# A decoder trunk on eight cores: engine orders and PSUM banks from a list schedule, and a packed layout from the host

## The chip, the cores and the metric

One Trainium2 chip, all 8 of its cores (two dies of four). Each core runs the same program on one prompt of 2048 tokens and on 16 sample sequences of 8 tokens; the cores do not talk to each other. The metric is the device time of the slowest core in microseconds, over separate executions. In the views PE is TensorE (matmuls), PEld its weight loads, DVE VectorE, ACT ScalarE, POOL GpSimd and SP SyncE; PSUM is the memory that PE writes to (`psum` in the views); both programs divide it into eight banks of 512 f32 columns.

## The reference, cut to what matters

Four layers. In each, `h` is a modulated RMS norm of `x`:

```python
def swiglu(h, wg, wu, wd):                    # 1024 -> 2816 -> 1024, twice per layer
    return (silu(h @ wg) * (h @ wu)) @ wd

def token_mixer(h, ...):                      # between the two FFNs
    xp, xl, gl, u, v, gates = split(h @ w_in) # 1024, 1024, 1024, 512, 512, 3 x 1024 wide
    y_pool = pool_mixer(xp)       # running means of 2, 4, 8, 16 tokens minus xp, times 256x256 blocks
    xc     = causal_conv(xl)      # 4 taps per channel
    y_lru  = rg_lru(xc) * gelu(gl)# two 128x128 gates per head, sigmoid, exp, sqrt(1 - a^2), a scan in time
    y_gm   = u * spatial_gate(v)  # RMS norm of v, then 128x128 causal mixing of positions
    g = sigmoid(gates)
    merged = g0*(y_pool @ wbo_pool) + g1*(y_lru @ wbo_lru) + g2*(y_gm @ wbo_gmlp)
    return merged @ w_out

mod = silu(c) @ w_ada + b_ada     # 9 x 1024 modulation values per layer (adaLN), 17 columns per core
```

The new pooling, convolution and recurrent states, and the normed `v` of the samples, are outputs too. The tokens go in two groups: group A is two prompt tiles of 512 tokens, group B two more and the sample tile of 128.

## The kernel before

Weights come from HBM as f32 and are cast to bf16 into a ring of 4 slots. A recorder works out semaphores from overlapping reads and writes; **each engine runs its operations in the order in which the code recorded them**, so the code itself is the schedule. What matters of it:

```python
class Sched:
    def add(self, eng, fn, reads=(), writes=(), dma=False):
        ...                              # dependencies from 512-byte pages last written and read
        self.ops[eng].append(o)          # the engine's order is the recorded order

psrot = {"mm": [0, 1, 2, 3], "aux": [4, 5], "tr": [6, 7]}   # PSUM banks, three rotations
def ps(pool="mm"): ...                   # the next bank of that rotation
SCRW = 10240
scr = sb("scr", [P, SCRW])               # one scratch area, cut by hand at fixed offsets

def lru_A(ch, t, par, wxl, wgl, wr_, wi_):   # one recurrent unit: a channel block of a tile
    U = BASE + par * 3344                # par = unit number % 2: two fixed scratch sets
    ...                                  # xl matmuls, 5 conv operations, the cast xcb, gl matmuls
    def stage_b():                       # put off by ONE unit, by hand
        mm(pr, wr_, xcb); mm(pi, wi_, xcb)     # the two gate matmuls that need the cast
        ...                              # gelu, tanh, tanh, exp, exp, ln, exp, two products, scan
        tt(ybr[:, ch, cols], xcf, gel, ALU.mult)
    return stage_b

# in mixer(): three branches one after the other, all through the buffer ybr
#   pooling -> gate_merge(0) -> recurrence -> gate_merge(1) -> gMLP -> gate_merge(2) -> w_out
def store_rows(src_fn, ncols, dram_rows):    # states go out as rows: transposed on PE
    for kb in range(2):
        for k4 in range(4): tr(pt[0:ncols, ...], src_fn(kb * 4 + k4))
        act(stg[...], pt[0:ncols, :], AF.Copy)
    dma(dram_rows, stg[0:ncols, :])

def wload(parts):                        # at EVERY weight load (group A, in the FFNs) ...
    ...
    if ada_hook[0] is not None: ada_hook[0]()   # ... one adaLN block of 2 MB (as f32) is loaded and used too
```

## Time and profile before

| | before |
|---|---|
| runs ahead of the change, us | 10006, 10009, 10119 |
| span of the profiled execution, us | 9312.5 |
| PE busy, share of the span | 78% |
| floor of PE's work (worked out in the prediction), us | 6670 |

Read it so: PE's own work is 6670 us and the span is 9312, so some 2640 us are the time in which PE waits, runs at a lower granted clock (0.52 in the second window of the start, 0.75 and 0.77 in two recurrent windows), or transposes. The prediction below shows the head of the page, the windows and the waits. Only the DMA lines are added here, from the page of the kernel before (packets by size; then for the queue of weight loads packets, MB, and the time that its packets took as a share of 16 engines' span):

```profile
DMA packets 1057984, 581.21 MB, mean 62 GB/s; under 512 B 301317, under 2 KB 1047469, under 8 KB 1057418
...
q0 software_dynamic: 974976, 536.94, 44.5%
```

More than nine packets in ten belong to the queue of weight loads; they are rows of weight blocks, 1 KB or less as written in bf16 (536.94 MB in 974976 packets, 551 bytes in the mean).

### The profile page before, as it was taken

The numbers are of one execution on the slowest core, as the hardware profiler recorded it, in microseconds if no ns is written. First come the engines' busy times: TensorE is split into PE (matmuls) and PEld (weight loads), VectorE is DVE, ScalarE is ACT, GpSimd is POOL, SyncE is SP. The second block draws the span as 40 slices with busy tenths as digits, with TensorE's granted clock in tenths as the row PEclk, the third lists the DMA queues.
The fourth block names the chain that finished last, engine by engine and source line by source line (L and its number), as shares of the span: only waits on it lengthen the run. The fifth ranks groups of instructions, "written<-read, shape, count | busy, mean of one in ns | idle before, by whom it ended". The sixth has DMA issues, their size and how long they took to land.

```text
span 9312.5 us, 113738 instructions; the slowest of 8 cores (9178.1 to 9312.5 us)
## 1 busy us (share of the span) xinstructions
PE 7283.7 (78%) x38120; PEld 3496.2 (38%) x38854; DVE 3499.0 (38%) x6164; ACT 2885.6 (31%) x4619; POOL 891.6 (10%) x1076
## 2 busy tenths in 40 slices
PE   2976888679976898696865699866898667996688
PEld 1422443234432343243432344433444333443344
DVE  0254223632155223632236232354323453324632
ACT  2143222521234222522126122254222452223621
POOL 1110111101110110110001010010000100110000
PEclk7988999889988999897987899988999888997899
DMA  4833886336942654354433254322544323543233
GB/s 82 115 47 49 114 115 91 48 54 84 123 54 42 83 70 54 50 67 81 47 53 35 45 63 59 52 36 41 66 58 56 44 43 53 66 54 50 39 53 62
DMA packets 1057984, 581.21 MB, mean 62 GB/s; under 512 B 301317, under 2 KB 1047469, under 8 KB 1057418
## 3 DMA queue, kind: packets, MB, share of 16 engines
q0 software_dynamic: 974976, 536.94, 44.5%
q1 hardware_dynamic: 82442, 36.95, 1.7%
q8 instruction: 327, 5.36, 0.2%
q14 instruction: 239, 1.96, 0.1%
HBM read 1095.39 MB, written 15.25 MB: 119 GB/s over the span
## 4 chain that ended last, share of the span: by engine, by line
PE 64%; DVE 13%; ACT 7%; DMA 6%; issue 6%; another core or an unknown queue 2%; DVEq 0%; POOL 0%; ACTq 0%; SPq 0%; POOLq 0%
PE psum L327 63%; ACT scr L345 6%; DVE scr L361 5%; DMA ring<-w_ada 4%; DVE scr L348 4%; DVE scr L365 2%; ACT L345 1%; PE psum L333 1%; DVE scr L375 1%; DVE scr L356 1%; DMA scr<-xp 0%; DVEq L180 0%; DMA ring<-w_out 0%; DMA o_pool_s<-stg 0%
## 5 line engine op out<-in xcount | busy, mean ns | idle before, releaser
L327 PE MATMUL psum<-hT,ring 128*128 128x512 bf16 (+1 forms) x21972 | 4499.3, 362 | 395.5 <-DMA ring<-w_in 124.3
L327 PEld LDWEIGHTS psum<-hT,ring 128*128 128x128 bf16 x22400 | 2092.1, 102 | 2695.0 <-issue 772.0
L345 ACT ACTIVATE scr<-psum 128x512 f32<-128x512 f32 (+5 forms) x1941 | 998.8, 516 | 4319.4 <-PE psum L327 3905.5
L327 PE MATMUL psum<-merged,ring 128*128 128x512 bf16 (+1 forms) x6253 | 1306.0, 354 | 96.7 <-DVE scr L348 43.4
L327 PE MATMUL psum<-ybr,ring 128*128 128x512 bf16 (+1 forms) x5030 | 1150.5, 355 | 80.8 <-issue 38.6
L348 DVE TENSOR_TENSOR merged<-scr,psum 128x512 bf16<-128x512 f32 (+1 forms) x640 | 388.8, 608 | 1614.1 <-PE psum L327 1596.4
L327 PEld LDWEIGHTS psum<-merged,ring 128*128 128x128 bf16 x6400 | 594.4, 101 | 714.8 <-issue 129.7
L361 DVE SCALAR_TENSOR_TENSOR xT<-psum,modT,xT 128x512 f32<-128x512 f32 x640 | 474.3, 749 | 957.3 <-PE psum L327 957.3
L327 PE MATMUL psum<-scr,ring 128*128 128x512 bf16 (+1 forms) x598 | 200.2, 437 | 752.4 <-DVE scr L365 462.4
L327 PEld LDWEIGHTS psum<-ybr,ring 128*128 128x128 bf16 x5120 | 480.0, 100 | 589.5 <-issue 126.5
L345 ACT ACT_TABLE_LOAD x387 | 496.5, 1283 | 403.8 <-PE psum L327 356.9
L361 DVE SCALAR_TENSOR_TENSOR scr<-scr,psum 128x512 f32<-128x512 f32 x320 | 194.0, 606 | 714.0 <-PE psum L327 499.5
L382 POOL DMA_DIRECT2D ring<-ffn_w_gate x192 | 168.1, 876 | 2771.2 <-PE psum L327 2771.2
L345 ACT ACTIVATE scr<-xT 128x4096 bf16<-128x4096 f32 (+1 forms) x65 | 201.7, 3104 | 658.2 <-DVE xT L361 620.0
L348 DVE TENSOR_TENSOR scr<-xT,scr 128x512 f32<-128x512 f32 (+1 forms) x396 | 250.1, 701 | 404.3 <-ACT scr L345 404.3
L327 PEld LDWEIGHTS psum<-scr,ring 128*128 128x128 bf16 x640 | 60.3, 104 | 862.0 <-issue 844.7
L382 POOL DMA_DIRECT2D ring<-w_in x224 | 200.0, 895 | 1836.0 <-PE psum L327 1716.8
L348 DVE TENSOR_TENSOR ybr<-scr,psum 128x512 bf16<-128x512 f32 (+1 forms) x240 | 145.8, 608 | 597.7 <-PE psum L327 596.0
L361 DVE SCALAR_TENSOR_TENSOR scr<-scr 128x512 f32<-128x512 f32 (+3 forms) x400 | 280.5, 701 | 166.6 <-ACT scr L345 144.2
L361 DVE SCALAR_TENSOR_TENSOR scr<-scr,vecT 128x512 f32<-128x512 f32 (+1 forms) x480 | 322.3, 671 | 53.9 <-DVE scr L361 0.9
L327 PE MATMUL psum<-scr,onesb 128*128 128x512 bf16 (+1 forms) x509 | 150.4, 458 | 200.4 <-ACT scr L345 199.7
L345 ACT ACTIVATE hT<-scr,modT 128x512 bf16<-128x512 f32 x384 | 276.0, 801 | 44.2 <-DVE scr L348 44.2
(86 smaller groups left out, 3675.0 us busy)
## 6 DMA issues: line engine op xcount, KB each, us to landing
ring<-ffn_w_down POOLq DMA_DIRECT2D x128, 704.0 KB, 7.3
ring<-ffn_w_gate POOLq DMA_DIRECT2D x160, 512.0 KB, 6.5
ring<-ffn_w_up POOLq DMA_DIRECT2D x160, 512.0 KB, 8.7
ring<-w_ada POOLq DMA_DIRECT2D x72, 1024.0 KB, 14.0
ring<-w_in POOLq DMA_DIRECT2D x64, 1024.0 KB, 9.5
ring<-w_in POOLq DMA_DIRECT2D x128, 256.0 KB, 5.1
ring<-w_in POOLq DMA_DIRECT2D x32, 512.0 KB, 5.7
ring<-wbo_pool POOLq DMA_DIRECT2D x16, 1024.0 KB, 8.3
```

The lines of the kernel that those rows point to most:

```text
L327: S.add("pe", lambda e: e.matmul(out, lhsT=lhsT, rhs=rhs, start=start, stop=stop), reads=[lhsT, rhs], writes=[out])
L333: S.add("pe", lambda e: e.transpose(out, in_, idn), reads=[in_, idn], writes=[out])
L345: S.add("act", lambda e: e.activation(out=out, in_=in_, func=func, **kw), reads=rd, writes=wr)
L348: S.add(eng, lambda e: e.tensor_tensor(out=out, in0=in0, in1=in1, op=op), reads=[in0, in1], writes=[out])
L356: S.add(eng, lambda e: e.tensor_scalar(out=out, in0=in0, scalar1=s1, scalar2=s2, op0=op0, op1=op1), reads=rd, writes=[out])
L361: S.add(eng, lambda e: e.scalar_tensor_tensor(out=out, in0=in0, scalar=scalar, in1=in1, op0=op0, op1=op1), reads=rd, writes=[out])
L365: S.add(eng, lambda e: e.tensor_copy(out=out, in_=in_), reads=[in_], writes=[out])
L375: S.add("dve", lambda e: e.tensor_tensor_scan(out=out, data0=d0, data1=d1, initial=init, op0=ALU.mult, op1=ALU.add), reads=rd, writes=[out])
L382: fn = lambda e: e.dma_start(out=out, in_=in_)
```

## The change

The intent is to stop ordering engines by hand. The code still records operations, but each has a modelled cost, a whole accumulation is one PE operation, a PSUM bank is a placeholder, and a list scheduler plays the graph through and lets each engine take what is ready first. Around it, the mixer's recording mixes the branches, and the host does all layout. Its core, with cuts:

```diff
+class PV:                       # a PSUM value; its bank is bound while scheduling
+    bank = None; refs = 0
 class Sched:
+    DMA_BW, PE_LAT, SEM_LAT, TABLE, PATIENCE = 215.0, 210.0, 70.0, 1300.0, 5000.0
+    def schedule(self):         # event-driven list schedule, priority = recorded order
+        banks = list(range(8))
+        ...
+                    if e == "pe":    # first ready op; one that needs a new bank only if > 2 are free,
+                        ...          # or if it is the oldest one that still needs a bank
+                            if o.alloc is None or len(banks) > 2 or (banks and o is pending_alloc[pa]):
+                                pick = o
+                    elif e == "act": # first ready op that needs no other activation table,
+                        ...          # unless the oldest has waited over PATIENCE ns
+                    if o.alloc is not None:
+                        o.alloc.bank = banks.pop(0)
+                    self.ops[e].append(o)
-psrot = {"mm": [0, 1, 2, 3], "aux": [4, 5], "tr": [6, 7]}
-scr = sb("scr", [P, SCRW])
+sbufs = [sb("s%d" % i, [P, SBW]) for i in range(NSB)]     # 14 scratch buffers, handed round when freed
+merged, ybr, ylr = RB                                     # the recurrence writes to its own ylr

 def lru_unit(l, ch, t, wblk):
-    return stage_b                   # no putting off by hand any more
-    cp(xlc[:, :, 3:L], pb[...])
+    act(xl[:, :, 3:L], pb(...), AF.Copy)                  # some copies go from DVE to ACT
-    tt(ybr[:, ch, cols], xcf, gel, ALU.mult)
+    tt(ylr[:, ch, t.cols], xcf, gb.f(n), ALU.mult)

 def mixer(...):
+    for c, f in fg:                  # fg: pooling, gates 0, gMLP, gates 2, each with an estimated cost c
+        while i < len(lru_seq) and al / tot_l <= af / tot_f * 1.04:
+            lru_seq[i][1]()          # recurrent units spread among them in proportion
+            ...
+        f()
+    ...                              # gates 1 (on ylr), then w_out

 def ffn(...):
-    for half in range(2): ...        # down projection in two halves of 11, two residual additions
+    acc(py.c(n), [(w[:, j, :], hid(j)[:, t.cols]) for j in range(22)], n)
+    norms[id(t)].chunk(m)            # squares for the next norm, chunk by chunk

+ada_ctl["every"] = 2 if l == 0 else 3     # an adaLN block at every 2nd or 3rd weight load
-    tr(...)                               # all PE transposes of x, states and outputs
+def pack_weights(inp): ...                # host: every weight block as one contiguous row per partition
```

## The prediction

> **What bounds the kernel now.** I read the page first: its head, the busy times and the chain that ended last.
>
> ```profile
> span 9312.5 us, 113738 instructions; the slowest of 8 cores (9178.1 to 9312.5 us)
> ...
> PE 7283.7 (78%) x38120; PEld 3496.2 (38%) x38854; DVE 3499.0 (38%) x6164; ACT 2885.6 (31%) x4619; POOL 891.6 (10%) x1076
> ...
> PE 64%; DVE 13%; ACT 7%; DMA 6%; issue 6%; another core or an unknown queue 2%; DVEq 0%; POOL 0%; ACTq 0%; SPq 0%; POOLq 0%
> ```
>
> No engine but PE is near full, yet PE is only 64% of the chain: the rest is PE waiting. To see where, I read the busy time by windows of 100 us (columns: PE, PEld, DVE, ACT, POOL busy with counts, granted clock, DMA share, GB/s).
>
> ```profile
> 100.00:200.00 100.00, 12.56 (x207) 7.51 (x208) 10.26 (x18) 27.70 (x47) 7.01 (x8) 0.52 0.46 62
> ...
> 1100.00:1200.00 100.00, 86.87 (x554) 40.73 (x563) 17.76 (x25) 16.16 (x40) 17.70 (x20) 0.91 0.98 132
> ...
> 2800.00:2900.00 100.00, 53.29 (x163) 19.64 (x166) 72.71 (x125) 72.04 (x88) 4.62 (x6) 0.75 0.28 43
> ...
> 3200.00:3300.00 100.00, 99.53 (x457) 45.30 (x464) 23.58 (x33) 11.84 (x20) 12.60 (x14) 1.00 0.62 76
> ...
> 6200.00:6300.00 100.00, 49.07 (x213) 23.26 (x219) 77.41 (x171) 80.04 (x111) 7.93 (x11) 0.77 0.24 26
> ```
>
> Four regimes. The first 200 us hardly compute. An FFN stage without disturbance (3200) is perfect: 464 weight loads in 100 us, 215.5 ns for each 512-column matmul, clock 1.00. An FFN stage with adaLN weights beside it (1100) is held by DMA: share 0.98 at 132 GB/s. The recurrent stage (2800, 6200) runs DVE and ACT at 72 to 80% in one dependent chain; PE starves, and its clock falls to 0.75. The waits name the partners:
>
> ```profile
> PE psum L327 <- DVE scr L365: 482.1, 158, 8.2
> PE psum L327 <- ACT scr L345: 356.4, 115, 13.0
> PE psum L327 <- DVE scr L361: 230.3, 87, 9.1
> PE psum L327 <- DMA ring<-w_ada: 137.1, 32, 32.0
> PE psum L327 <- issue: 134.5, 48, 37.1
> PE psum L327 <- DMA ring<-w_in: 124.3, 4, 40.7
> ```
>
> The first and third are DVE work ahead of the small gate matmuls of the recurrent stage (the cast) and the pooling stage (the difference). PE stands behind them because its order is fixed by hand.
>
> **The floor.** The grouped instructions by form count weight loads, which are complete (matmul records miss 2%): 22400 on hT, 6400 on merged, 5120 on ybr, and so on. From the loop bounds: a 512-token tile needs 1056 matmuls of 512 columns for the two FFNs of a layer, 708 for the mixer, 24 for norms: 1788. Times 4 layers and 4 tiles, and the final norm: 28640, at 215.5 ns: 6172 us. The sample tile needs 7160 of 128 columns. In the dense window at 4500 there are 612 loads, a third of them of 128 columns: 408 x 215.5 = 88 us leaves 12 us for 204, 59 ns each: 422 us. adaLN's 2304 of 17 columns ran 32 in 1.07 us: 77 us. Sum **6670 us**. So 2640 of 9312 us are waits, half-clock time and transposes.
>
> [...] dense windows of all eight cores have 1.00. [...] the trace has 387 loads of 1283 ns[...].
>
> **The change, part by part.**
>
> *Mixer.* The windows put a mixer of the first token group (two tiles) at about 500 us (2600 to 3100) and of the second (with samples) at about 600 (5900 to 6500). PE's work there is 2 x 708 x 215.5 = 305 us, and 305 + 42 = 347 us. Loss 195 + 253, times 4 layers: **about 1790 us**, by far the largest. The change spreads the recurrent units over pooling, gating and gMLP, gives them a buffer of their own (ylr), draws PSUM banks from one pool of 8, and lets PE take any ready matmul. Can the others keep up? Per tile of 153 us of PE: DVE has recurrence 8 x 6.9 us (conv 0.57 + 3 x 0.75, cast 0.43, three of 0.69, scan 1.28, others), gates 40 x 0.69, pooling 28 x 0.7, gMLP 6, residual and norm 12: some 121 us, 79%. ACT has recurrence 8 x 5.6, gates 24 x 0.6, pooling 12, gMLP 6, norm and squares 12: 90 us, and 20 to 25 table loads x 1.28: about 120 us, 78%. Both fit, but two engines at 79% in chains of 15 us or more (five conv operations, cast, matmul, two tanh, load, three exp or ln, two products, scan), with 14 scratch buffers handed round in a fixed order, will not keep PE full, and a static order from modelled costs can't adapt. I choose 10% loss: 8 mixers x 33 = 260 us left, so **1530 won**.
>
> *FFN and norms.* Two FFNs of a layer are 455 us of PE (first group) and 455 + 62 (second); the windows show some 10% lost, half of it adaLN's transfers in the first two layers. Each weight load now draws one adaLN block of the same size: 2 MB in bf16 per 2 x 2 x 16 x 215.5 ns = 13.8 us, 152 GB/s, above the 132 at which the queues filled. Changed, one comes with every second or third load: 76 x 1.5 = 114 or 101 GB/s, under the limit. Squares by chunk replace one 3.6 us activation on the way to each norm. The down projection runs 22 deep: same matmuls, but 256 of the 640 residual operations of 0.75 us go (DVE 190 us lighter, off the path). I leave 100 us of loss: **about 300 won**.
>
> *Transposes, layout.* About 660 transposes go, with their evictions; their rows sum to about 165 us of PE and some 245 us of waits around them, partly in the start. Packed weights turn rows of 1 KB or less (1,047,469 of 1,057,984 packets are under 2 KB) into long ones; DMA: this helps only where DMA bound, counted above. **About 200 won**, outside the start.
>
> *Start and end.* The start loses about 230 us; 4 adaLN blocks and x directly in place leave about 60: **170 won**. Between groups and at the end some 60 us stay.
>
> Sum of what stays: 6670 + 260 + 100 + 60 + 60 = 7150 us of span (9312 - 1530 - 300 - 200 - 170 gives 7112: the same within my reading of windows).
>
> **From span to the time.** The timed runs before are 10009, 697 us above the profiled span, and no view tells why. *Offset:* 7150 + 697 = 7850. *Ratio:* 7150 x 1.075 = 7690. [...] I weigh offset and ratio at 55%[...], and say **8050 us**.
>
> **Rivals.** (1) *Denser PE, lower clock*[...]: for it, [...]the unexplained 697; against it, clock 1.00 in all eight cores' dense windows. [...] (2) *ACT and DVE become the bound of the mixer*: for it, 79% each, and greedy table switching: with ACT often idle, whatever is ready next switches the set. 100 more loads per mixer than I count is 128 us of ACT; PE busy in mixers stays near 75%, and 100 us more in each of 8: span 7900, time about 8650. Against it: PSUM lets PE run ahead four gate units of 3.45 us. (3) *The static order misjudges DMA*: its model gives 215 GB/s of f32; the trace's ceiling is 264. If arrivals still come late, waits of 10 us at 40 loads give 400 us: 8450. (4) *Nearly perfect*: PE at 97%, span 6900, time 7420 to 7600.
>
> **Range and chances.** Rival 4 with the ratio bounds below, 2[...] above: **7550 to 8600**. To miss a 2% gain (9810) almost all of the mixer's gain would have to vanish. Faster 0.97, same 0.02, slower 0.01.
>
> **What would show it.** Right: span 6900 to 7500 with PE busy over 90%; mixer windows over 85% with DVE and ACT near 80%; waits of PE on DVE under 200 us in all; no wait on w_ada; first dense window before 100 us; transposes gone; DVE busy about 3200. [...] Wrong: mixer windows still near 60% with ACT or DVE over 90%, or table loads well above 500, or PE waiting on its weights.

## The result, and the profile after

| | before | after |
|---|---|---|
| all runs, us | 10119.39, 10009.47, 10006.14, 9342.6 | 7267.68, 7265.08, 8006.48, 8108.1 |
| median, us | 10007.81 | 7637.08 |
| fast runs, us | 9342.6 | 7267.68, 7265.08 |
| profiled span, us | 9312.5 | 7266.1 |
| PE busy | 78% | 93% |

The change is **faster**: the ratio of fast runs is 0.780 (95% interval 0.772 to 0.787). The fast runs as listed give 7266/9343 = 0.778. The median of 7637 is between two fast runs and two slow ones; in the two slow ones die 1 took 7946 to 8107 us at a clock of 0.85 to 0.87, while die 0 took 7248 to 7268 as in the fast ones. **The effect of the change is 9343 to 7266.**

The page of the kernel after (head, busy times, DMA, and the chain of work that ended last):

```profile
span 7266.1 us, 107436 instructions; the slowest of 8 cores (7247.2 to 7266.1 us)
...
PE 6735.0 (93%) x37489; PEld 3290.5 (45%) x38200; DVE 3001.6 (41%) x5604; ACT 2800.3 (39%) x4853; POOL 408.0 (6%) x793
...
DMA packets 127533, 593.11 MB, mean 82 GB/s; under 512 B 15648, under 2 KB 35232, under 8 KB 85024
...
q0 software_dynamic: 89856, 539.01, 42.4%
...
PE 83%; ACT 6%; issue 5%; DVE 4%; DMA 1%; SPq 1%; POOL 0%; ACTq 0%; DVEq 0%; POOLq 0%
```

PE is now 83% of the chain where it was 64%. There are 8 times fewer packets, yet the queue's share of the span hardly fell, from 44.5 to 42.4%, of a span that is 22% shorter: keep that in mind for experiment e4. The matmul count, 37489, is 711 short of the weight loads, 38200; in the trace of experiment e4, with the same weight loads, both counts are 38200, so the trace here lacks 2% of the matmul records.

The busy time by windows of the kernel after, core 0 (start:end, length, then busy us with counts of PE, PEld, DVE, ACT and POOL, granted clock, DMA share, GB/s):

```profile
0.00:100.00 100.00, 45.67 (x319) 20.74 (x324) 19.11 (x47) 33.79 (x57) 8.38 (x36) 1.00 0.81 157
1000.00:1100.00 100.00, 99.42 (x540) 46.69 (x549) 19.93 (x32) 15.59 (x26) 7.47 (x13) 1.00 0.52 92
2800.00:2900.00 100.00, 81.38 (x355) 35.51 (x360) 60.17 (x119) 59.55 (x103) 5.33 (x9) 0.93 0.29 51
2900.00:3000.00 100.00, 90.20 (x403) 40.47 (x412) 66.94 (x119) 70.02 (x111) 7.02 (x14) 0.93 0.41 71
3400.00:3500.00 100.00, 59.77 (x308) 27.29 (x312) 30.48 (x49) 40.01 (x70) 1.58 (x3) 0.78 0.54 136
4700.00:4800.00 100.00, 69.73 (x396) 35.04 (x401) 77.13 (x166) 62.66 (x128) 3.75 (x6) 0.88 0.34 76
```

The four regimes of before have changed unequally. The start costs half a window instead of two; the first FFN matmul runs at 65 us. An FFN stage with adaLN beside it (1000) is as dense as one without: 99.42, DMA share 0.52. The mixers (2800, 2900, 4700) still lose time, though 10 to 30% of a window where it was 47 to 51. The change of groups (3400) loses 40 us.

Adding up 100 minus PE's busy time over all windows of each kind gives where PE still stands:

| us lost | kernel after | expected to be left |
|---|---|---|
| mixers of group A (4) | 153 | |
| mixers of group B (4) | 236 | |
| mixers together | 389 | 260 |
| FFN stages and norms | 34 | 100 |
| start | 54 | 60 |
| change of groups, end | 40 + 14 | 60 |
| PE busy above the floor (6735 − 6670), put down to the low clock after stops | 65 | 0 |
| sum, with the floor of 6670 | 7266 | 7150 |

The 34 is mostly an artefact: a dense window reads 99.4 here and 100.00 in a trace that lacks no matmul records (experiment e4), so about 0.5% of the span belongs to busy PE time rather than to the FFNs.

The waits of PE in the kernel after, core 0 (who waits, for what; us in total, times, longest):

```profile
PE psum L491 <- ACT s L513: 116.0, 67, 21.8
PE psum L491 <- DVE s L521: 92.3, 13, 11.2
PE psum L491 <- DVE s L542: 61.8, 21, 16.1
...
PE psum L491 <- DMA ring<-ffn_gu: 11.4, 1, 11.4
...
PE psum L491 <- DMA ring<-ada_w: 5.6, 1, 5.6
```

The cast (a copy on DVE, L542) cost PE 482 us before and costs 62 now, or 109 with the waits put down to the copies of the recurrent state (`lrust`, 47.6 us), which come from the same helper line. The line next to it, DVE additions of the pooling stage (L521), is 13 waits of 7 us on average and 11 at most: once or twice in each mixer. The timeline of PE in the kernel after shows one of these:

```profile
4753.58 1.86 PE L491 MATMUL psum<-hT,ring 128*128 128x128 bf16 x16 [1.73 <-ACT s L513]
4766.27 1.48 PE L491 MATMUL psum<-s,ring 128*128 128x512 bf16 x3 [10.82 <-DVE s L521]
4768.10 1.86 PE L491 MATMUL psum<-s,ring 128*128 128x512 bf16 x4 [0.35 <-DVE s L536]
...
4771.81 1.89 PE L491 MATMUL psum<-R,ring 128*128 128x512 bf16 x8
```

The next in PE's list are the pooling matmuls on the scratch buffer, and they wait 10.8 us for DVE's chain of additions. The list is fixed when the program is built, so PE cannot turn to something else. The clock is low after this stop: the granted clock reads 0.50 from 4766 to 4770 us, 0.90 from 4770 to 4772 and 1.00 from there to 4778. Four matmuls take 1.86 us (465 ns each, against 215.5 in dense windows), and some 3.5 us later eight of the same size take 1.89 us (the window at 4700 has 0.88).

### The profile page after: what moved, and what is told of

The parts are those of the page before. It is cut to its first block, busy times and chain, and to the rows that moved or that the text cites. A ratio compares the mean times of both kernels' runs of the same rounds, so it can differ in the third digit from the quotient of the medians.

```text
span 7266.1 us, 107436 instructions; the slowest of 8 cores (7247.2 to 7266.1 us)
## 1 busy us (share of the span) xinstructions
PE 6735.0 (93%) x37489; PEld 3290.5 (45%) x38200; DVE 3001.6 (41%) x5604; ACT 2800.3 (39%) x4853; POOL 408.0 (6%) x793
## 3 DMA queue, kind: packets, MB, share of 16 engines
q0 software_dynamic: 89856, 539.01, 42.4%
## 4 chain that ended last, share of the span: by engine, by line
PE 83%; ACT 6%; issue 5%; DVE 4%; DMA 1%; SPq 1%; POOL 0%; ACTq 0%; DVEq 0%; POOLq 0%
PE psum L491 83%; ACT s L513 4%; ACT L513 1%; DVE s L536 1%; DVE s L521 1%; DVE s L551 1%; SPq L558 1%; ACT R L513 1%; DVE R L521 0%; POOL small L521 0%; DMA y_p<-s 0%; DMA xT<-xp 0%; DVE s L542 0%; DMA ring<-ffn_gu 0%; ACT hT L513 0%
## 5 line engine op out<-in xcount | busy, mean ns | idle before, releaser
L491 PE MATMUL psum<-R,ring 128*128 128x512 bf16 (+1 forms) x11319 | 2216.5, 347 | 28.1 <-ACT s L513 15.7
L513 ACT ACTIVATE s<-psum 128x512 f32<-128x512 f32 (+1 forms) x1905 | 996.8, 535 | 2852.7 <-PE psum L491 2652.2
L491 PEld LDWEIGHTS psum<-R,ring 128*128 128x128 bf16 x11520 | 1034.6, 98 | 1104.9 <-issue 28.5
L521 DVE TENSOR_TENSOR R<-s,psum 128x512 bf16<-128x512 f32 (+1 forms) x880 | 534.0, 608 | 1982.6 <-PE psum L491 1928.5
L513 ACT ACTIVATE s<-xT 128x512 bf16<-128x512 f32 (+1 forms) x520 | 287.9, 562 | 1166.4 <-DVE xT L536 1067.5
L513 ACT ACT_TABLE_LOAD x386 | 495.2, 1283 | 197.2 <-PE psum L491 128.7
L536 DVE SCALAR_TENSOR_TENSOR s<-s 128x512 f32<-128x512 f32 (+3 forms) x480 | 290.6, 609 | 319.4 <-ACT s L513 311.6
L536 DVE SCALAR_TENSOR_TENSOR s<-s,vecT 128x512 f32<-128x512 f32 (+1 forms) x480 | 319.3, 669 | 28.9
L521 DVE TENSOR_TENSOR s<-xT,s 128x512 f32<-128x512 f32 x408 | 252.2, 686 | 101.1 <-ACT s L513 85.2
L513 ACT ACTIVATE hT<-s,modT 128x512 bf16<-128x512 f32 x384 | 276.6, 801 | 25.7 <-DVE s L521 23.8
L521 DVE TENSOR_TENSOR s<-s 128x526 f32<-128x526 f32 (+7 forms) x400 | 244.8, 651 | 38.1 <-ACT poolst L513 27.5
```

The source lines that it names most:

```text
L491: ins = e.matmul(res(o), lhsT=l, rhs=r, start=st, stop=sp)
L513: return S.add("act", lambda e: e.activation(out=res(out), in_=res(in_), func=func, **kw), reads=rd, writes=wr, cost=cost, tset=TSETS.get( ...
L521: return S.add(eng, lambda e: e.tensor_tensor(out=res(out), in0=res(in0), in1=res(in1), op=op), reads=[in0, in1], writes=[out], cost=dcost(n))
L536: return S.add(eng, lambda e: e.scalar_tensor_tensor(out=res(out), in0=res(in0), scalar=scalar, in1=res(in1), op0=op0, op1=op1), reads=rd, ...
```

## The experiments

All kernels below compute the right result. **Spans of the slowest core** (of the undisturbed die where a run was slow) are compared with the 7266 of after. They ran on four chips in four batches; the fast runs of the kernel before, on three chips, were 9343, 9304 and 9292, so a difference of under some 50 us between batches is not taken as shown.

The theory was that the order of issue is the cause: hand-ordered PE stands behind chains of DVE and ACT, and a list schedule lets it do other work meanwhile. Rivals: the mixed recording of the branches does it, whatever orders the engines; the layout and the DMA do it; or banks and buffers do it.

### e1: the recorded order back, everything else as changed

```diff
 def schedule(self):
+    for o in self.all:                 # engines in recorded order; banks from the same pool of 8
+        if o.alloc is not None:
+            o.alloc.bank = banks.pop(0); ...
+        self.ops[o.eng].append(o)
+def schedule_list(self):               # the list schedule, unused
```

> The changed kernel with its engine orders taken from the order in which the program records its operations; banks from a free list of 8 in that order; everything else as changed. Theory A (the list order is what fills PE): PE stops at each recurrent unit for the conv chain and at each pooling unit for its adds, some 35 to 90 us for each of 18 tile-layers, FFN windows stay dense: span 8000 to 8900, PE busy in the mixers 55 to 70%. Rival (the hand-made mixing of the branches and the layout do the work, the order of issue adds little): span below 7500.

Measured: a fast run of 9713, span 9711 (a second run was slow, its undisturbed die at 9686 to 9706). Page, waits and windows of this kernel:

```profile
span 9711.3 us, 107673 instructions; the slowest of 8 cores (9683.1 to 9711.3 us)
...
PE 7182.3 (74%) x37502; PEld 3415.8 (35%) x38200; DVE 3123.9 (32%) x5604; ACT 2876.4 (30%) x4837; POOL 401.2 (4%) x793
```

```profile
PE psum L510 <- DVE s L561: 1405.7, 212, 14.7
PE psum L510 <- ACT s L532: 569.8, 258, 17.8
...
PE psum L510 <- DMA ring<-ada_w: 105.3, 11, 21.1
```

```profile
2600.00:2700.00 100.00, 49.42 (x194) 19.67 (x198) 44.38 (x82) 35.00 (x57) 1.59 (x3) 0.74 0.10 18
3100.00:3200.00 100.00, 99.49 (x512) 46.18 (x520) 23.32 (x37) 22.89 (x37) 4.77 (x9) 1.00 0.52 94
```

The order, with the banks bound along it, is worth **2445 us** here, more than the whole change, and the rival of the mixed recording falls. The changed kernel in its recorded order is even slower than the kernel before: PE waits 1406 us for the cast of the recurrent unit (L561) because the gate matmuls now follow it with only the eight `gl` matmuls between, the putting off by one unit being gone. So the 2445 us compare the list schedule with an order that nobody tuned by hand. How much of them a hand-made order with the putting off would win back on this graph was not tested. The mixer window at 2600 has PE, DVE and ACT all under 50%: one chain, one after the other. The FFN window at 3100 is as dense as ever.

### e2: the list schedule, but the branches recorded one after the other

```diff
-        for c, f in fg:
-            while i < len(lru_seq) and al / tot_l <= af / tot_f * 1.04: ...
+        for _, f in fg[:n01]: f()          # pooling, gates 0
+        for _, f in lru_seq: f()           # recurrence, gates 1
+        ...
+        for _, f in fg[n01:]: f()          # gMLP, gates 2
```

> The changed kernel with the list schedule, but the mixer recorded branch after branch (pooling and its gates, recurrence and its gates, gMLP and its gates) as before. Theory A (look-ahead is bounded by 8 banks and 14 scratch buffers, so the recorded mixing is needed as well): the recurrent stage is again held by ACT and DVE, some 65 us for a tile against 31 of PE; span 7500 to 7900. Rival (the list schedule finds the mixing itself): span 7200 to 7350.

Measured: a fast run of 7413, span 7411: **+145 us**. The scheduler finds most of the overlap by itself; the mixing by hand adds a smaller part. My theory expected more of it.

### e3: both undone

This is e1's edit and e2's together.

> Recorded order and branches in turn. What is left of the change is layout, start, adaLN spacing, norms by chunk. By my working that keeps some 600 of the 2050 us: span 8600 to 9100, and more if the missing hand-made deferral by one unit costs more than that. If layout had brought most of the gain: below 7900.

Measured: three runs, all slow; in two of them one die was undisturbed, and its cores took 9788 to 9824. So without a list schedule the mixing is worth about 100 us (9711 against about 9810) and with it 145: the two hardly interact. The number expected was far too low, because I had taken this kernel for one like that before; it lacks the putting off by hand, for which the expectation had only left room.

### e11: the kernel before with a list schedule alone

The converse: before's code, its three bank rotations, its fixed scratch sets and all its transposes, with nothing but the engine orders taken from the same list scheduler.

```diff
 # against the kernel BEFORE
 class Sched:
+    def schedule(self): ...               # the same list schedule; banks and scratch stay as recorded
 def finalize(self, nc, stack):
+    self.schedule()
```

> The kernel before, with nothing changed but the order in which each engine issues its operations, taken from the same list scheduler (same constants); banks stay in the fixed rotations of 4, 2 and 2, scratch in pairs, transposes, row layout, adaLN at every load, FFN in halves as they were. Reference: 9312 (its undisturbed profile). If order alone is the cause of the gain: 7600 to 8000. If fixed banks and paired scratch bound the look-ahead, so that order needs them changed as well: 8300 to 8900. If the hand-made order was already as good as these buffers allow: 9100 to 9400.

Measured: a fast run of 9028 against 9304 of the kernel before in the same batch: **−276 us**, no more, between the second and the third range expected. Page, waits and windows of this kernel:

```profile
span 9026.2 us, 114641 instructions; the slowest of 8 cores (9004.0 to 9026.2 us)
...
PE 7155.3 (79%) x38854; PEld 3419.0 (38%) x38854; DVE 3419.5 (38%) x6164; ACT 2871.2 (32%) x4635; POOL 888.2 (10%) x1076
```

```profile
PE psum L440 <- DVE scr L478: 757.4, 112, 14.0
...
PE psum L440 <- DMA ring<-w_ada: 3.6, 1, 3.6
```

```profile
400.00:500.00 100.00, 0.00 (x0) 0.00 (x0) 0.00 (x0) 0.00 (x0) 0.00 (x0) 0.50 0.07 20
2600.00:2700.00 100.00, 98.50 (x655) 47.71 (x654) 20.99 (x31) 20.84 (x50) 18.04 (x20) 1.00 1.18 150
2900.00:3000.00 100.00, 38.35 (x144) 15.00 (x144) 59.15 (x107) 67.14 (x82) 5.71 (x8) 0.70 0.21 28
```

Two things happen. The start became worse: nothing computes in the window at 400, PE is all but idle until 501 us, and the first FFN matmul runs at 532, where it ran at 202 in the kernel before. PE waits there for rows of `x` and `c` (82.7 and 88.6 us, one wait each); the scheduler has put 256 small transfers (a block-diagonal matrix, `BD`) into the first 510 us, of which the kernel before has none ahead of its first FFN matmul. Without that (my estimate from these two times, some 330 us) the order would have won about 600. And in the mixer PE still stands: 757 us behind the cast, and the window at 2900 has PE at 38%. So **the order is not a cause by itself**. It seems to need a graph that allows another order: here the scheduler can only move within what fixed banks, two fixed scratch sets and the recording branch by branch leave open. Which of these holds it, this run does not show. Between this kernel and after lie 1760 us.

One thing the order does by itself: PE waits 3.6 us for adaLN weights here, where the kernel before waited 137, with the same rows and a block at every load. In e1, with packed rows and the blocks spaced out but in recorded order, 105 us of these waits are there.

### e10: the list order, but banks bound in recorded order

```diff
 def schedule(self):
+    for o in self.all:                    # banks handed out in recorded order, before scheduling;
+        if o.alloc is not None:           # their reuse becomes an ordinary dependency
+            o.alloc.bank = banks.pop(0); o.deps += last users of that bank
+            o.alloc = None
```

> The changed kernel with its list order, but each PSUM tile bound to a bank in recorded order (free list of 8) ahead of the scheduling, so that PE cannot pass an older tile that waits for the same bank. If choosing banks in the schedule matters: 7350 to 7600. If the order alone does the work: within 40 us of 7266.

Measured: both runs slow; in the first, die 1 was undisturbed at 7356 to 7375 us, median 7367.5 against 7256 of after's dies: about **+110 us**. Binding banks while scheduling, not before, is worth that; against the dies of e8b below (medians 7240 and 7236), on the same chip, it is some 130, a part of which is e8b's own difference from after. The slow die of the same run shows what that state is (core 0, a dense FFN window, then the medians of the dies):

```profile
3700.00:3800.00 100.00, 99.29 (x375) 41.41 (x382) 14.71 (x21) 12.13 (x20) 4.23 (x8) 0.81 0.33 58
```

```profile
die 0 (median of its cores): 8423.8 us, clock 0.821
die 1 (median of its cores): 7367.5 us, clock 0.967
```

The same program does 382 weight loads in 100 us on this die, 262 ns for each matmul instead of 215.5, at a clock of 0.81. In the second run both dies were so: 8570 to 8610 us.

### e12: one branch buffer, as before, in the scheduled kernel

e2's edit, and the recurrence writes to `ybr` again instead of `ylr`; the gMLP values get a buffer of their own (cut here).

```diff
-        tt(ylr[:, ch, t.cols], xcf, gb.f(n), ALU.mult)
+        tt(ybr[:, ch, t.cols], xcf, gb.f(n), ALU.mult)
-                mk_gate(1, m, t, KC, ylr)()
+                mk_gate(1, m, t, KC, ybr)()
```

> Branches in turn with the list schedule, and the recurrent branch writes its results where the pooling branch did (one branch buffer, as in the kernel before, in place of two); the gMLP value tiles have a buffer of their own so that they are no tighter than before. Reference: branches in turn alone, 7408. If the second buffer is what lets the schedule lay the recurrence beside the pooling gates: the recurrent stage is again alone with some 60 us of ACT and DVE against 31 of PE for a tile: 7800 to 8200. If scratch and banks carry the overlap and the buffer matters little: 7400 to 7550.

Measured: 7436, span 7435: **+23** against e2, too little to be called shown. In the scheduled kernel one buffer for the branches costs next to nothing, so it is an unlikely reason for what held e11; in before's own graph it was not tested.

### e4, e5, e6: packing and adaLN

e4 loads the weights from the reference's own layout (rows of 128 to 512 columns, so packets of 256 bytes to 1 KB in bf16, in the trace of e4 438 bytes in the mean); e5 puts adaLN blocks back at every weight load; e6 does both.

```diff
-    ada_w = din("ada_w", [NL, 18, P, 4096])                      # e4, e6: and so for every weight
+    ada_w = Src(lambda l, s: [(0, KC, wc(r_ada[l], s * 512, 512))])   # 8 rows for each partition
-                ada_ctl["every"] = 2 if l == 0 else 3            # e5, e6
+                ada_ctl["every"] = 1
```

> The changed kernel with the weights in the reference's layout: the same blocks in the same order, but read as rows of 256 or 128 columns (1 KB or 512 B). Everything else as changed. Theory (packing matters only where DMA is near its limit): FFN gate and up blocks need 76 GB/s, with adaLN 101 to 114, under the 132 at which the kernel before filled its queues; down blocks of 512 B rows need 74[...]: span 7300 to 7450, waits of PE on ring blocks 40 to 180 us. Rival A (packing brought a large part): above 7600. Rival B (no matter at all): within 20 us of 7266.

> The changed kernel (packed) with one adaLN block at every weight load in place of every second or third. If the packed rows lifted the DMA ceiling (157 GB/s at share 0.81 in the first window, so some 190), the 145 to 152 GB/s asked for are met: within 30 us of 7266. If the spacing was what removed the adaLN waits: 80 to 200 us longer, with waits of PE on ada_w.

> Rows unpacked and adaLN at every load, as the kernel before had both. 145 to 152 GB/s asked for against 132: the FFN windows of the first layers at DMA share 0.95 or more and PE at 85 to 90% there, as before; 100 to 250 us over the kernel with rows unpacked alone.

Measured, in one batch: e4 7247.5, e5 7321, e6 7313. DMA lines of the page of e4:

```profile
DMA packets 1269049, 593.25 MB, mean 82 GB/s; under 512 B 531488, under 2 KB 1255584, under 8 KB 1268512
...
q0 software_dynamic: 1231360, 539.04, 63.0%
```

Windows of e6, core 1:

```profile
100.00:200.00 100.00, 98.69 (x627) 47.45 (x626) 20.57 (x35) 16.12 (x27) 17.05 (x20) 1.00 1.19 149
1000.00:1100.00 100.00, 98.08 (x617) 46.83 (x615) 19.88 (x34) 16.12 (x27) 17.48 (x20) 0.98 1.16 150
```

**Packing is worth nothing to the time.** Ten times the packets take the queue from 42 to 63% of the engines' time, but those engines were not on the path (DMA is 2% of e4's chain that ended last), and e4 is not slower than after (19 us lower, within the spread). On one chip, with adaLN at every load, e5 (packed, 7321) and e6 (not packed, 7313) say the same. adaLN at every load costs 65 us with short rows (e6 against e4, the same chip) and some 55 packed (e5 against after). And even then short rows carry 149 to 150 GB/s beside PE at 98%, as they do in e11's window at 2600: the 132 GB/s at which I saw before's queues full is no ceiling of the transfers. Nor did a DMA share of 0.98 mean full: the same column reads 1.16 to 1.19 here.

### e9: the transposes back

```diff
+    def dummy_tr(reads, ntr, evict): ...  # ntr f32 transposes into one bank and one ACT copy of them
 def load_x(t):
+    dummy_tr([xT[:, k, ...] for i in range(t.n // P)], t.n // P, t.n)
 # and so at the final norm and, for the sample group, in each mixer: 624 transposes in all
```

They transpose data that is there already, and their result is not used, so this measures PE's and ACT's time and the banks, not the waits for rows.

> The changed kernel with 624 transposes of 128x128 f32 put back (136 of the inputs, 136 of the outputs, 88 for the states in each of 4 layers) with their evictions, their results unused. Prediction's term: about 200 us for transposes and layout. If they cost PE time alone, 0.2 us each: 125 us, span 7390; if their waits come back as well: 7450 to 7500; if they hide in PE's gaps: 7290 to 7330.

Measured: 7354.6, span 7353: **+87 us**, 0.14 us for each transpose. It is less than the 125 us that PE time alone was expected to cost; that some of them fall into waits is my explanation, not shown.

### e7, e8b: what the mixers still lose

e7 counts pooling as nearly free in the proportions, so that more recurrent units are recorded after the pooling stage, not in it. e8b adds to it an own buffer for the gMLP values, whose matmuls depend on nothing but `hT`, and mixes them among the pooling units.

```diff
-                    fg.append((4.3 if t.kind == "p" else 1.2, mk_pool(g, t)))
+                    fg.append((0.4 if t.kind == "p" else 0.1, mk_pool(g, t)))
 # e8b as well:
-    vnT = ybr[:, 4:8, :].rearrange("p a b -> p (a b)")
+    vnT = vnb_t[:]                        # a buffer of its own
```

> The changed kernel, but pooling units count little in the pacing of the recurrent units (0.4 in place of 4.3), so that few recurrent units fall into the pooling stage, where DVE is at 77% and PE at 70 to 80%. Theory (DVE is the bound in the pooling stage, and later stages have room): span 7266 less 80 to 150. Rival (PE waits there for latency, norm or a misjudged order): within 20 us of 7266, or longer by 50 when the recurrence ends late and holds up its gates.

> A better version is tried: pacing as in the earlier run, and the gMLP value tiles in a buffer of their own, so that their matmuls (7 us of PE for a tile, no DVE) can be mixed among the pooling units, where PE stood still for DVE. If PE lacked DVE-free work there: 7130 to 7190. If the loss is the norm at the mixer's start or the static order: 7220 to 7260.

Measured: e7 7234, span 7232.5 (−34); e8b 7252, span 7251 (−15). One mixer window of e7, core 3, and below it the same window and core of after (core 0, shown above, had 90.20):

```profile
2900.00:3000.00 100.00, 97.20 (x464) 44.21 (x462) 64.21 (x108) 77.53 (x124) 15.84 (x29) 1.00 0.48 85
...
2900.00:3000.00 100.00, 93.91 (x426) 42.00 (x427) 64.10 (x114) 71.89 (x114) 8.21 (x18) 0.95 0.40 71
```

That window got a little denser, yet of 80 to 150 us expected only 34 came, within the spread; feeding PE more independent work in the pooling stage did not bring more. What binds the remaining 49 us in each mixer is not settled. No version clearly beats the changed kernel.

## Why the prediction was right or wrong

**Right: the mechanism.** PE stood behind dependent chains because its order was fixed by hand. Undoing the order in the new kernel brings back 2445 us (e1), though an unmeasured part of that may be the putting off by hand, which the recorded order lacks; and the waits by name fell as foreseen (the cast from 482 to 62 us). What the prediction did not separate is that the order needs the rest of the change: alone it won 276 (e11).

**Mis-sized: what the mixers keep.** I expected 260 us and 389 stayed; group A's mixers lose 38 each, close to the 33 I had put, group B's 59. PE's waits for DVE come to 236 us over all lines, not under 200, and those for ACT to 228, some of them in the start and at the change of groups. The rival "ACT and DVE become the bound" is only half met: in the mixer windows where PE is under 90% DVE is at 50 to 79% and ACT at 55 to 75%, not above 90, and table loads are 386 against 387, of 1283 ns each; but the longest stops inside the mixers, up to 16 us, are on DVE.

**Mis-sized: the FFNs.** I left 100 us; 34 is the reading and most of that is missing records. This offsets most of what the mixers lost more.

**Left out: the low clock after a stop.** PE's busy time is 65 us over the floor, and more if the missing records are counted. After the stop of 10.8 us in the timeline above, matmuls took about twice their time (465 ns against 215.5, at a granted clock of 0.50) for some 3.5 us, and my sum had no term for it. That all 65 us are this was not worked out matmul by matmul. With these three, 7150 + 129 − 66 + 65 − 12 (start, middle, end) is 7266.

**Wrong: the DMA step.** I took 132 GB/s at a share of 0.98 (264 as f32, in rival 3) as the limit of the transfers and derived from it what adaLN's spacing and packing would win. e6 and e11 carry 150 GB/s with the same short rows and PE at 98%, and e4 shows packing worth nothing. The spacing is worth some 55 to 65 us, the packing none. What took PE's 137 us of waits for adaLN weights away is mostly the order: 3.6 are left with the order alone (e11), 105 with packing and spacing but in recorded order (e1).

**Mis-sized: transposes and layout**, 200 us predicted. In the scheduled kernel transposes cost 87 (e9) and packing is worth nothing. In before's order, where each stood in a fixed place, they may have cost more; that was not measured alone.

**Right: start, middle and end.** 54 and 54 us stay where 60 and 60 were expected. The gain at the start is smaller than my 170: the first FFN matmul runs at 65 us instead of 202, 137 earlier.

**Wrong: from span to time.** I took the 697 us between before's profile and its runs for something that the changed kernel would also pay, and so put 8050 where the span was 7150. It was a difference of state: the three runs were slow and the profile fast. A fourth run took 9343, later ones 9304 and 9292, and in fast runs time and span differ by under 2 us (7267.68 and 7266.1). The number to compare with fast runs was 7150, which is 1.6% below them; 8050 is 11% above, and a fast run of 7266 lies below the whole range. That the median, 7637, lies in the range is luck: it is the mix of two fast and two slow runs.

**The lower-clock rival is real, but a state and not a rule.** The weight it had in the 8050 rested on a clock that no trace had shown by then. A slow die shows 0.81 and 262 ns for each matmul in a dense window (e10), and with both dies slow the cores of e10, itself 110 us longer than after, took 8570 to 8610 at a mean clock of 0.80. In the profiled fast run of after each of the eight cores has 33 or 34 windows of 100 us with PE busy over 98.9%, all at 1.00.

**What the gain is made of, and what stays open.** Taken out of the scheduled kernel one at a time: the mixed recording 145, banks bound while scheduling 110, transposes 87, adaLN's spacing about 55, the own branch buffer 23 (within the spread), packing 0; the start, by its first FFN matmul, 137. Together this is about 560 us, if such terms may be added, which no run shows. The list order is worth 2445 on the new graph and 276 on the old, so most of the gain is in the two together. Between e11 and after there are 1760 us, less some 330 for e11's bad start, less the 560; some 870 belong to what I did not test alone: scratch buffers handed round instead of two fixed sets, eight banks in one pool instead of 4, 2 and 2, whole accumulations as one operation, copies moved from DVE to ACT, the weight ring handed out by size instead of in 4 slots, and the FFN in one piece. The fixed scratch sets are my first suspect, since e11's waits are still for the cast into one; that is argued, not shown.

## What to carry to other kernels

When several engines work in dependent chains and none is full, take the orders from a list schedule of the whole graph, but free the graph first: the same scheduler won 276 us over a hand-made order on fixed banks and scratch sets, and over 2400 on a graph without them, there against an order that nobody had tuned. Ask of every layout or DMA improvement whether the transfers are on the path at all; packing cut the packets tenfold (e4 against after) and the time did not change. And before explaining a gap between a profile and a time, look at whether both ran in the same state.
